# Two gated linear attentions in one decoder layer: how the scans' scores are placed and how the values are turned

## Chip, cores and metric

The kernel runs on one core of a Trainium2 chip. The metric is the device time of one execution in microseconds. Before the change the median of three runs is 2266.98 us (2266.93 to 2267.67). In what follows PE is TensorE, DVE is VectorE, ACT is ScalarE, POOL is GpSimd, and SP is the engine whose queue issues most loads.

## What is computed

One layer of a decoder for a prompt of 256 tokens and 8 samples of 4 new tokens (32 columns), 288 columns in all, at width 2048: a gated feed-forward part (FFN, inner width 5632), a mixer, and a second FFN, each between two norms. The mixer is a linear recurrence per head, four GLA heads (values 256 wide) and eight HGRN2 heads (values 128 wide):

```python
x = x + 0.5 * rmsnorm(swiglu(rmsnorm(x, g[0]), ffn1_w_in[l], ffn1_w_out[l]), g[1])
m, sg, sh = hybrid_mixer(rmsnorm(x, g[2]), ...)
x = x + rmsnorm(m, g[3])
x = x + 0.5 * rmsnorm(swiglu(rmsnorm(x, g[4]), ffn2_w_in[l], ffn2_w_out[l]), g[5])

# in the mixer, per head:
#   S_t = diag(exp(log_a_t)) S_{t-1} + k_t^T v_t ;  o_t = q_t S_t
```

The outputs are the layer's result for all tokens and the heads' new states.

## The kernel before

**Layout and matmuls.** Activations lie with features on the 128 partitions and the 288 tokens along the free axis: 16 tiles x (the residual), 16 tiles y (outputs of a part, later the heads' outputs), and xh and xl, the high and low halves of the normed input. Every large product is made of three matmuls of 288 columns (lines 548 to 550): high weights with both halves of the input, low weights with the high half. `block` does such a product for 512 output rows; a `tick` is called after each of its 16 steps over the inner dimension, that is after 12 matmuls. Weights come through SP in units of 128 x 1024; ACT copies the high half of a unit (wh, line 96) and DVE subtracts it from the raw one (wl, line 97).

**The mixer.** Its blocks in order are qk0, v0, qk1, v1 (GLA), hfq0, hi0, hfq1, hi1, hfq2, hfq3 (HGRN2), four gate blocks, and the output projection. A scan handles two heads; there are six scans (two GLA, four HGRN2). A scan is a Python generator; each tick of a later block runs one step of it (`step`), so its small operations stand between the block's matmuls in program order on each engine. A GLA scan skips the first four ticks of a block (SCAN_LAG). Each engine works through its own queue in that order.

**A scan.** The scores of a scan are built level by level (level lv pairs blocks of h = 2**lv tokens, masks and decay products F by `update`, lines 1022 to 1027). Step 0 makes own, the elementwise product of q and k at even tokens, in the tile rp, split in halves oh and ol. At step 2 `score01` sums own over the features by two 288-column matmuls with a matrix of ones (line 975, into sc_o) and makes levels 0 and 1 by `quarters` (line 959): blocks of 32 by 32 tokens on four column groups of PE. At step 3 `put01` moves them into Dg, the 2 x 2 tiles of 128 x 128 scores, by DVE's copy_predicated under the mask mk; `put_masked` (line 968) does one such copy for each of four partition blocks of 32, since each block's destination lies in other columns of Dg. At step 4 follow the sample scores into Ds (lines 1001, 1009) and `put23` (three times `put_masked`). Level 4 (h = 16) is copied by ACT (line 1080, four copies), levels 5 and 6 by ACT too (line 1086), level 7 into X. The steps with an extra yield are 3 to 6: scores are made at one tick and put at the next. After the levels come key_t, `out` (lines 1168 to 1178, the outputs from Vt, Dg, X, the states and Ds), the norm, the new states (line 1205) and their stores through POOL's queue (line 1207).

**The values.** A value block (v0, v1, hi0, hi1) leaves its product times rt in y tiles, and the 32 sample columns three times in v3 (lines 887, 888). Its four `turn`s wait in the list `turns`; one is taken at each tick of the next block from k = 1 on. A turn makes three PE transposes (`by_token`, lines 866 and 867) into tp_v; ACT copies the two prompt ones into Vt (line 895) and the sample one into V32 (line 896), and `stack` makes the high and low halves Vs (lines 871, 873).

**The other place that matters.** The last FFN turns its results already by `turn32` (line 660: DVE's block transposes of 32 x 32) and `move32` (lines 671, 675): 20 DMAs on POOL's queue put the blocks where a full transpose would have them.

Of the kernel before, what the change touches and what calls it, by code (L numbers as in the profile page):

```python
# [9 lines left out]
F32 = mybir.dt.float32  # L10
F32R = mybir.dt.float32r
# [5 lines left out]
P = 128  # L17
# [108 lines left out]
def trunk_kernel(ctx, tc, x_prompt, x_sample, state_gla, state_hgrn, norm_gains, f1_in, f1_out, f2_in, f2_out,  # L126
# [116 lines left out]
    y = [xpool.tile([P, T], F32, name=f"y{k}") for k in range(KT)]  # L243
# [532 lines left out]
    def mixer(pn, border):  # L776
        with ExitStack() as mx:
# [15 lines left out]
            mk = cst.tile([P, 576], U8, name="mk")  # L793
# [27 lines left out]
            def setup():  # L821
# [20 lines left out]
                G.tensor_copy(mk, mi32)  # L842
# [20 lines left out]
            def by_token(tp, src, src3):  # L863

                for t in range(2):
                    PE.transpose(tp[:, t * P:(t + 1) * P], src[:, t * P:(t + 1) * P], ident)
                PE.transpose(tp[0:96, TP:TP + P], src3, ident)
# [7 lines left out]
            def vtiles(nm):  # L875
                vs32.append(vs32.pop(0))
                return (gp.tile([P, 2, 512], F32, name=f"V{nm}", tag="V"), vs32[-1],
                        gp.tile([96, 512], F32R, name=f"Vs{nm}", tag="Vs"))
# [3 lines left out]
            def ev_v(Vt, V32, Vs, y0=8):  # L882
                def ev(f, ps):

                    vt = y[y0 + f]
                    v3 = tmp.tile([P, 3, TS], F32, name="v3", tag="v3", bufs=4)
                    V.tensor_tensor(vt[:, 0:TP], ps[:, 0:TP], rt[:, 0:TP], op=ALU.mult)
                    V.tensor_tensor(v3, ps[:, TP:T].unsqueeze(1).broadcast_to([P, 3, TS]),
                                    rt[:, TP:T].unsqueeze(1).broadcast_to([P, 3, TS]), op=ALU.mult)

                    def turn():
                        tp = auxtile("tp_v")
                        by_token(tp, vt, v3.rearrange("p n t -> p (n t)"))
                        c = slice(f * P, (f + 1) * P)
                        S.activation(Vt[:, 0:2, c], tp[:, 0:TP].rearrange("p (t c) -> p t c", c=P), AF.Copy)
                        S.activation(V32[0:TS, c], tp[0:TS, TP:TP + P], AF.Copy)
                        stack(Vs[:, c], tp, TS)

                    turns.append(turn)
                return ev  # L900
# [9 lines left out]
            def scan(d, Vt, V32, Vs, gla, ytile0, s0, sp_out, ss_out):  # L910
# [34 lines left out]
                oh = sp[0].tile([P, T], F32R, name="oh", tag="bd")  # L945
                ol = sp[0].tile([P, T], F32R, name="ol", tag="bd")
# [15 lines left out]
                def put_masked(src, h, m):  # L962

                    for b in range(4):
                        r = slice(b * TS, (b + 1) * TS)
                        dst = Dflat[r, :, r].rearrange("p j (n two k) -> p j n two k", two=2, k=h)[:, :, :, 1, :]
                        mv = mk[r, m * 64 + b * 16:m * 64 + (b + 1) * 16].rearrange("p (n k) -> p n k", k=h)
                        V.copy_predicated(dst, mv.unsqueeze(1).broadcast_to(dst.shape),
                                          src[r].rearrange("p j (n k) -> p j n k", k=h))

                def score01():

                    ps, po = auxtile("sc01"), auxtile("sc_o")
                    for i, part in enumerate((oh, ol)):
                        PE.matmul(po[:, 0:T], ones[128], part, start=i == 0, stop=i == 1, skip_group_check=True)
                    quarters(ps, lambda i, a, b: R[:, a, :, i * 64 + b * 16:i * 64 + (b + 1) * 16])
                    for a in range(2):
                        c = T + a * TS
                        PE.matmul(po[0:TS, c:c + TS], k[:, a, TP:T], R[:, a, :, P:P + TS // 2],
                                  start=False, stop=True, skip_group_check=True)  # L980
                    return ps, po

                def put01(ps, po):
                    def eye(n, m):
                        return mk[0:n, 448:448 + 2 * m].rearrange("p (n two) -> p n two", two=2)[:, :, 0]

                    def odd():
                        for lv in range(2):
                            put_masked(ps[:, 0:P].rearrange("p (j l c) -> p j l c", j=4, l=2)[:, :, lv], 1 << lv, lv)

                    def even():
                        v = Dflat.rearrange("p (i a) (n two) -> p i a n two", a=2, two=2)
                        ov = po[:, 0:T].rearrange("p (a c) -> p a c", a=2)
                        for i in range(2):
                            V.copy_predicated(v[:, i, :, :, 0], eye(P, 64).unsqueeze(1).broadcast_to([P, 2, 64]),
                                              ov[:, :, i * 64:(i + 1) * 64])

                    def sampled():
                        sv = Ds[0:TS].rearrange("p a (n two) -> p a n two", two=2)
                        ov = po[:, 0:T].rearrange("p (a c) -> p a c", a=2)  # L1000
                        V.copy_predicated(sv[:, :, :, 0], eye(TS, 16).unsqueeze(1).broadcast_to([TS, 2, 16]),
                                          ov[0:TS, :, P:])
                        for lv in range(2):
                            h = 1 << lv
                            m = mk[:, lv * 64:(lv + 1) * 64]
                            dst = Ds[0:TS].rearrange("p a (n two k) -> p a n two k", two=2, k=h)[:, :, :, 1, :]
                            for a in range(2):
                                c = T + a * TS + lv * 16
                                V.copy_predicated(dst[:, a], m[0:TS, 0:16].rearrange("p (n k) -> p n k", k=h),
                                                  po[0:TS, c:c + 16].rearrange("p (n k) -> p n k", k=h))  # L1010

                    return [odd, even, sampled]
# [60 lines left out]
                def put(lv, ps):  # L1073
# [17 lines left out]
                for step in range(LEVELS + 1):  # L1091
                    if step == 0:
                        V.scalar_tensor_tensor(own.unsqueeze(3), halves(q, 1, False), 128.0, halves(k, 1, False),
                                               op0=ALU.mult, op1=ALU.mult)
                        S.activation(oh, rp, AF.Copy)
                        V.tensor_tensor(Q, q, d["f"], op=ALU.mult)
                        V.tensor_tensor(ol, rp, oh.bitcast(F32), op=ALU.subtract)
# [425 lines left out]
```

## Time and profile before

| what | value |
|---|---|
| median of the runs shown | 2266.98 us |
| the profiled execution, its own time | 2267.07 us |
| its span, first to last instruction | 2265.0 us |
| mean granted TensorE clock | 0.998 |
| ACT busy, copies of wh (line 96) | 711.5 us |
| DVE busy, subtractions of wl (line 97) | 821.7 us |
| weights moved by SP's queue (q1) | 365.15 MB, 50.6% of 16 DMA engines |
| POOL's queue (q0) | 14.41 MB, 2.4% |

Busy times of different engines overlap. A row of a group gives line, engine, operation, out<-in, shapes and count; then busy time and the mean duration of one in ns; then the idle time of the engine just before such operations and what ended it. In a timeline a row is start, duration, engine, line, operation, and in brackets the wait ahead of it with its releaser. A PE row's duration is the latency of a matmul, not the step from one to the next, since matmuls are pipelined.

### The profile page before, as it was taken

The page shows a single profiled execution, that of the slowest core. Times are in us where ns is not written, and L with a number is a line of the kernel's source. Part 1 is how long each engine was busy: PE and PEld are TensorE (multiplying, and loading weights), DVE is VectorE, ACT ScalarE, POOL GpSimd, SP SyncE. Part 2 cuts the span into 40 slices and gives each one's busy share as a digit, 9 for nine tenths or more (in the row PEclk, how much of TensorE's full clock was granted, in tenths as well). Part 3 has the DMA queues.
Part 4 walks back from the last instruction along what each step waited for, and adds up shares of the span by engine and source line. Part 5 has one row for each costly group of instructions (what it writes and reads, how often), then busy time and mean ns, then how long its engine had stood idle before and what let it go on. Part 6 is the DMA issues. An engine that isn't in the chain of part 4 may idle for free. (4 is left out here: it accounts for less than half of the span.)

```text
span 2265.0 us, 43259 instructions
## 1 busy us (share of the span) xinstructions
PE 2244.5 (99%) x17760; PEld 2227.3 (98%) x17760; DVE 1409.0 (62%) x2359; ACT 1022.7 (45%) x1581; POOL 134.9 (6%) x241
## 2 busy tenths in 40 slices
PE   9999999999999999999999999999999999999998
PEld 9999999999999999999999999999999999999998
DVE  6545545554555468888889754954555455545546
ACT  6443333333334346555656654644333333333344
POOL 2000000000000001011000000440000000000005
PEclk9999999999999999999999999999999999999999
DMA  6555555555555554566555554565555555555545
GB/s 213 171 165 167 168 167 163 165 167 168 167 164 182 167 168 140 168 187 189 163 167 177 164 186 150 168 190 165 164 167 167 168 164 164 165 168 168 164 164 156
DMA packets 225605, 382.49 MB, mean 169 GB/s; under 512 B 20242, under 2 KB 60224, under 8 KB 225408
## 3 DMA queue, kind: packets, MB, share of 16 engines
q1 hardware_dynamic: 214736, 365.15, 50.6%
q0 software_dynamic: 8496, 14.41, 2.4%
q8 instruction: 139, 2.28, 0.4%
q10 hardware_dynamic: 2176, 0.18, 0.1%
q14 instruction: 58, 0.48, 0.1%
HBM read 363.75 MB, written 11.80 MB: 166 GB/s over the span
## 5 line engine op out<-in xcount | busy, mean ns | idle before, releaser
L97 DVE TENSOR_TENSOR wl<-raw,wh 128x1024 fp32r<-128x1024 f32 (+1 forms) x674 | 821.7, 1220 | 615.3 <-ACT wh L96 612.7
L96 ACT ACTIVATE wh<-raw 128x1024 fp32r<-128x1024 f32 (+1 forms) x674 | 711.5, 1057 | 1018.9 <-PE gate L549 313.7
L548 PE MATMUL gate<-xh,wh 128*128 128x288 f32 x1660 | 488.4, 296 | 0.6 <-ACT xh L254 0.6
L550 PE MATMUL gate<-xh,wl 128*128 128x288 f32 x1660 | 488.5, 295 | 0.4 <-DVE wl L97 0.4
L549 PE MATMUL gate<-xl,wh 128*128 128x288 f32 x1660 | 485.7, 295 | 0.6 <-DVE xl L255 0.6
L549 PE MATMUL out<-hl,wh 128*128 128x288 f32 x1408 | 415.7, 295 | 0.0
L550 PE MATMUL up<-xh,wl 128*128 128x288 f32 x1408 | 415.0, 295 | 0.0
L550 PE MATMUL out<-hh,wl 128*128 128x288 f32 x1408 | 415.0, 295 | 0.0
L548 PE MATMUL up<-xh,wh 128*128 128x288 f32 x1408 | 414.9, 295 | 0.0
L549 PE MATMUL up<-xl,wh 128*128 128x288 f32 x1408 | 414.6, 294 | 0.0
L548 PE MATMUL out<-hh,wh 128*128 128x288 f32 x1408 | 413.7, 294 | 0.0
L548 PEld LDWEIGHTS gate<-xh,wh 128*128 128x128 f32 x1660 | 310.9, 188 | 1.9 <-ACT xh L254 1.0
L550 PEld LDWEIGHTS gate<-xh,wl 128*128 128x128 f32 x1660 | 311.3, 188 | 1.1 <-DVE wl L97 0.8
L549 PEld LDWEIGHTS gate<-xl,wh 128*128 128x128 f32 x1660 | 310.4, 188 | 1.2 <-DVE xl L255 0.8
L550 PEld LDWEIGHTS out<-hh,wl 128*128 128x128 f32 x1408 | 264.7, 188 | 0.0
L548 PEld LDWEIGHTS out<-hh,wh 128*128 128x128 f32 x1408 | 264.6, 188 | 0.0
L549 PEld LDWEIGHTS out<-hl,wh 128*128 128x128 f32 x1408 | 264.4, 188 | 0.0
L548 PEld LDWEIGHTS up<-xh,wh 128*128 128x128 f32 x1408 | 264.1, 188 | 0.3
L549 PEld LDWEIGHTS up<-xl,wh 128*128 128x128 f32 x1408 | 264.2, 188 | 0.1
L550 PEld LDWEIGHTS up<-xh,wl 128*128 128x128 f32 x1408 | 264.2, 188 | 0.0
L706 DVE TENSOR_TENSOR y<-out,y 128x288 f32<-128x288 f32 x288 | 121.2, 452 | 101.3 <-PE out L550 98.3
L548 PE MATMUL hfq<-xh,wh 128*128 128x288 f32 x256 | 77.6, 304 | 0.0
(376 smaller groups left out, 2518.9 us busy)
## 6 DMA issues: line engine op xcount, KB each, us to landing
raw<-in_ffn_w_in_dram SPq DMA_DIRECT2D x351, 512.0 KB, 3.5
raw<-in_ffn_w_out_dram SPq DMA_DIRECT2D x176, 512.0 KB, 3.5
raw<-in_mix_w_in_dram SPq DMA_DIRECT2D x64, 512.0 KB, 3.8
raw<-in_mix_w_in_dram SPq DMA_DIRECT2D x96, 256.0 KB, 3.1
raw<-in_mix_w_out_dram SPq DMA_DIRECT2D x32, 512.0 KB, 3.6
out_dram<-s POOLq DMA_DIRECT2D x32, 256.0 KB, 2.8
s<-in_state_gla_dram SPq DMA_DIRECT2D x16, 256.0 KB, 4.2
s<-in_state_hgrn_dram SPq DMA_DIRECT2D x16, 256.0 KB, 4.2
```

The lines of the kernel that those rows point to most:

```text
L96: i1 = self.nc.scalar.activation(h[:, c], raw[:, c], AF.Copy).ins
L97: i2 = self.nc.vector.tensor_tensor(l[:, c], raw[:, c], h[:, c].bitcast(F32), op=ALU.subtract).ins
L548: yield lambda: PE.matmul(dst, w[0][:, c:c + P], parts[0], start=start, stop=False)
L549: yield lambda: PE.matmul(dst, w[0][:, c:c + P], parts[1], start=False, stop=False)
L550: yield lambda: PE.matmul(dst, w[1][:, c:c + P], parts[0], start=False, stop=stop)
L706: V.tensor_tensor(y[k], ps, y[k], op=ALU.add)
```

## The change

Three things move together.

- Masked copies: a new tile Db of 128 x 4 x 32 holds, for each partition block, only its own 32 columns. `put_masked` writes it for all 128 partitions in one copy, with masks rearranged so that each partition block finds its own 16 columns; the diagonal (even) scores and level 4 go the same way. At step 6, `place` copies Db into Dg by four ACT copies.
- score01: own is summed by matmuls with a 128 x 32 tile of ones, block by block, as the scores are; oh, ol and the tile sc_o go. All of it shares one PSUM tile.
- Values: for v0, v1 and hi0 the PE transposes are replaced by DVE block transposes into four y tiles that are free at that time (spare), and 20 DMAs on POOL's queue; then `parts` makes Vs from V32. hi1 has no spare tiles and keeps PE (`by_engine`). The 16 y tiles become four groups of four, Vt is laid out as [128, 4, 2, 128], and the entries of `turns` for a turned block are eight: two block transposes, four moves, an empty one, parts.

```diff
-    y = [xpool.tile([P, T], F32, name=f"y{k}") for k in range(KT)]
+    yg = [xpool.tile([P, 4, T], F32, name=f"y{k}") for k in range(4)]
+    y = [yg[k // 4][:, k % 4, :] for k in range(KT)]
...
-            mk = cst.tile([P, 576], U8, name="mk")
+            mk = cst.tile([P, 8, 16], U8, name="mk")
+            one32 = cst.tile([P, TS], F32, name="one32")
+            Db = cst.tile([P, 4, TS], F32, name="Db")
...
-                G.tensor_copy(mk, mi32)
+                G.memset(one32, 1.0)
+                G.memset(Db, 0.0)
+                for b in range(4):
+                    r = slice(b * TS, (b + 1) * TS)
+                    G.tensor_copy(mk[r, 0:7], mi32[r, 0:448].rearrange("p (l c) -> p l c", c=64)[:, :, b * 16:(b + 1) * 16])
+                    G.tensor_copy(mk[r, 7], mi32[r, 448 + b * TS:448 + (b + 1) * TS]
+                                  .rearrange("p (n two) -> p n two", two=2)[:, :, 0])
...
-            def ev_v(Vt, V32, Vs, y0=8):
+            def ev_v(Vt, V32, Vs, g, spare):
+                vg = yg[g]
+                if spare is not None:
+                    flat = yg[spare].rearrange("p f c -> p (f c)")
+                    b32 = flat[:, 0:4 * TP].rearrange("p (q n c) -> p q n c", q=4, c=TS)
+                    bs32 = flat[:, 4 * TP:].rearrange("p (f c) -> p f c", c=TS)
+                def by_engine(f):
+                    def run():
+                        tp = auxtile("tp_v")
+                        by_token(tp, vg[:, f, :])
+                        S.activation(Vt[:, f], tp[:, 0:TP].rearrange("p (t c) -> p t c", c=P), AF.Copy)
+                        S.activation(V32[0:TS, f * P:(f + 1) * P], tp[0:TS, TP:TP + P], AF.Copy)
+                    return run
+                def turn32(f):
+                    def run():
+                        for i in (f, f + 1):
+                            V.transpose(b32[:, :, 2 * i:2 * i + 2, :], vg[:, i, 0:TP].rearrange("p (t q c) -> p q t c", t=2, q=4))
+                        if f:
+                            V.transpose(bs32, vg[:, :, TP:T])
+                    return run
+                def move32(b, sample):
+                    rows = cols = slice(b * TS, (b + 1) * TS)
+                    def run():
+                        if sample:
+                            for n in range(4):
+                                r = slice(n * TS, (n + 1) * TS)
+                                G.dma_start(V32[0:TS].rearrange("p (f c) -> p f c", c=P)[:, :, r], bs32[r])
+                        for q in range(4):
+                            G.dma_start(Vt[q * TS:(q + 1) * TS, :, :, cols].rearrange("p f t c -> p (f t) c"), b32[rows, q])
+                    return run
+                def parts():
+                    v = V32[0:TS, :]
+                    S.activation(Vs[0:TS, :], v, AF.Copy)
+                    V.tensor_tensor(Vs[TS:2 * TS, :], v, Vs[0:TS, :].bitcast(F32), op=ALU.subtract)
+                    S.activation(Vs[2 * TS:96, :], v, AF.Copy)
                 def ev(f, ps):
...
+                    V.tensor_tensor(vg[:, f, :], ps, rt, op=ALU.mult)
+                    if spare is None:
+                        turns.append(by_engine(f))
+                    if f == 3:
+                        if spare is not None:
+                            turns.append(turn32(0))
+                            turns.append(turn32(2))
+                            turns.extend(move32(b, b == 0) for b in range(4))
+                            turns.append(lambda: None)
+                        turns.append(parts)
...
                 def put_masked(src, h, m):
-                    for b in range(4):
...
+                    dst = Db.rearrange("p j (n two k) -> p j n two k", two=2, k=h)[:, :, :, 1, :]
+                    mv = mk[:, m, :].rearrange("p (n k) -> p n k", k=h)
+                    V.copy_predicated(dst, mv.unsqueeze(1).broadcast_to(dst.shape),
+                                      src.rearrange("p j (n k) -> p j n k", k=h))
+                def place():
+                    for b in range(4):
+                        r = slice(b * TS, (b + 1) * TS)
+                        S.activation(Dflat[r, :, r], Db[r], AF.Copy)
                 def score01():
-                    ps, po = auxtile("sc01"), auxtile("sc_o")
-                    for i, part in enumerate((oh, ol)):
-                        PE.matmul(po[:, 0:T], ones[128], part, start=i == 0, stop=i == 1, skip_group_check=True)
+                    ps = auxtile("sc01")
                     quarters(ps, lambda i, a, b: R[:, a, :, i * 64 + b * 16:i * 64 + (b + 1) * 16])
+                    v = ps[:, P:P + 64].rearrange("p (i a c) -> p i a c", i=2, a=2)
                     for a in range(2):
+                        for b in range(4):
+                            PE.matmul(v[b * TS:(b + 1) * TS, :, a, :], one32,
+                                      own[:, a, 0:P].rearrange("p (i c) -> p i c", i=2)[:, :, b * 16:(b + 1) * 16],
+                                      start=False, stop=True, skip_group_check=True)
+                    for a in range(2):
+                        c = 192 + a * 16
+                        PE.matmul(ps[0:TS, c:c + 16], one32, own[:, a, P:P + 16],
+                                  start=False, stop=True, skip_group_check=True)
...
+                def put01(ps):
+                    for lv in range(2):
+                        put_masked(ps[:, 0:P].rearrange("p (j l c) -> p j l c", j=4, l=2)[:, :, lv], 1 << lv, lv)
+                    dst = Db.rearrange("p j (n two) -> p j n two", two=2)[:, :, :, 0]
+                    V.copy_predicated(dst, mk[:, 7, :].unsqueeze(1).broadcast_to(dst.shape),
+                                      ps[:, P:P + 64].rearrange("p (j c) -> p j c", j=4))
+                def put01_sample(ps):
+                    dst = Ds[0:TS].rearrange("p a (n two) -> p a n two", two=2)[:, :, :, 0]
...
+                    for lv in range(2):
...
+                        V.copy_predicated(dst, mv.unsqueeze(1).broadcast_to(dst.shape), src)
...
                     elif h == 16:
-                        for b in range(0, P, TS):
-                            S.activation(Dflat[b:b + h, :, b + h:b + TS],
-                                         ps[b:b + h, 0:64].rearrange("p (j c) -> p j c", j=4), AF.Copy)
+                        put_masked(ps[:, 0:64].rearrange("p (j c) -> p j c", j=4), h, lv)
...
                     if step == 0:
-                        V.scalar_tensor_tensor(own.unsqueeze(3), halves(q, 1, False), 128.0, halves(k, 1, False),
-                                               op0=ALU.mult, op1=ALU.mult)
-                        S.activation(oh, rp, AF.Copy)
+                        V.tensor_tensor(own.unsqueeze(3), halves(q, 1, False), halves(k, 1, False), op=ALU.mult)
                         V.tensor_tensor(Q, q, d["f"], op=ALU.mult)
-                        V.tensor_tensor(ol, rp, oh.bitcast(F32), op=ALU.subtract)
...
                         if step == 3:
-                            odd, even, sampled = put01(*pss.pop(1))
-                            odd()
-                            even()
+                            put01(pss[1])
                         elif step == 4:
-                            sampled()
+                            put01_sample(pss.pop(1))
                             put23(*pss.pop(3))
                         else:
                             put(step - 1, pss.pop(step - 1))
+                            if step == 6:
+                                place()
...
-                    block("v0", KT, xrhs, ev_v(*vt), 
+                    block("v0", KT, xrhs, ev_v(*vt, 2, 1), 
...
-                    block("v1", KT, xrhs, ev_v(*vt), tick=tick)
+                    block("v1", KT, xrhs, ev_v(*vt, 2, 1), tick=tick)
...
-                    block(f"hi{g}", KT, xrhs, ev_v(*vts[g], 8 + 4 * g), tick=tick)
+                    block(f"hi{g}", KT, xrhs, ev_v(*vts[g], 2 + g, None if g else 3), tick=tick)
```

More of the change, by code (lines that the diff above doesn't have):

```diff
@@ L861, in group_tiles, with by_token @@
                 return {n: gp.tile([P, 2, T], F32, name=f"{n}_{nm}", tag=n) for n in ("q", "k", "f")}
-            def by_token(tp, src, src3):
+            def by_token(tp, src, src3=None):
                 for t in range(2):
                     PE.transpose(tp[:, t * P:(t + 1) * P], src[:, t * P:(t + 1) * P], ident)
-                PE.transpose(tp[0:96, TP:TP + P], src3, ident)
+                n = TS if src3 is None else 3 * TS
+                PE.transpose(tp[0:n, TP:TP + P], src[:, TP:T] if src3 is None else src3, ident)
             def stack(dst, tp, low):
@@ L876, in vtiles @@
                 vs32.append(vs32.pop(0))
-                return (gp.tile([P, 2, 512], F32, name=f"V{nm}", tag="V"), vs32[-1],
+                return (gp.tile([P, 4, 2, P], F32, name=f"V{nm}", tag="V"), vs32[-1],
                         gp.tile([96, 512], F32R, name=f"Vs{nm}", tag="Vs"))
             turns = []
-            def ev_v(Vt, V32, Vs, y0=8):
-                def ev(f, ps):
[L885 to L899, printed above, removed]
```

54 lines of the change are left out of this document (14 added, 40 removed).

## The prediction

> **What bounds the kernel now.** I read the page's busy times first, then the windows over the mixer, then the PE and VectorE timelines around the places where PE stands.
>
> ```profile
> span 2265.0 us, 43259 instructions
> PE 2244.5 (99%) x17760; PEld 2227.3 (98%) x17760; DVE 1409.0 (62%) x2359; ACT 1022.7 (45%) x1581; POOL 134.9 (6%) x241
> ```
>
> PE works 99% of the span. So the time is the matmul stream plus its holes: an edit gains only if it takes instructions from PE or closes a hole, and anything on VectorE, ScalarE or GpSimd is free until PE waits for it. The holes of the mixer, where all of the change lies, show in windows laid over it (columns: microseconds, then busy time of PE, weight loads, DVE, ACT, POOL; five of fourteen windows and their sum):
>
> ```profile
> 1000.00:1030.00 30.00, 30.00 (x324) 28.50 (x324) 24.96 (x60) 19.37 (x44) 0.15 (x1) 1.00 0.64 194
> ...
> 1055.00:1085.00 30.00, 28.26 (x345) 26.89 (x343) 25.65 (x69) 15.16 (x39) 0.00 (x0) 1.00 0.61 175
> ...
> 1110.00:1130.00 20.00, 17.64 (x184) 16.44 (x184) 18.99 (x54) 9.23 (x27) 0.00 (x0) 1.00 0.45 137
> ...
> 1170.00:1215.00 45.00, 43.72 (x477) 41.97 (x476) 41.26 (x102) 28.50 (x69) 4.11 (x6) 1.00 0.57 171
> 1215.00:1260.00 45.00, 43.71 (x458) 42.19 (x457) 42.17 (x104) 28.67 (x68) 0.00 (x0) 1.00 0.54 161
> sum 435.00, PE 427.38 PEld 412.98 DVE 377.33 ACT 264.43 POOL 42.49; mean PE 30.53 PEld 29.50 DVE 26.95 ACT 18.89 POOL 3.03
> ```
>
> PE is short of full by 435.00 - 427.38 = 7.6 us, and nearly all of it (1.7, 2.4, 1.3, 1.3) lies in windows where DVE is busy 86 to 95%. Where DVE has air, as in 1000 to 1030, PE has no hole. What DVE does just ahead of two holes, and who waits, stands in the two timelines:
>
> ```profile
> 1114.45 3.04 DVE L968 COPY_PREDICATED Dg<-mk,sc 32x64 f32<-32x64 uint8 x12
> 1117.52 1.23 DVE L97 TENSOR_TENSOR wl<-raw,wh 128x1024 fp32r<-128x1024 f32 x1
> ...
> 1070.85 0.33 PE L1069 MATMUL sc<-Q,k_h 128*32 128x32 f32 x16 [1.30 <-DVE F L1027]
> ...
> 1118.80 0.40 PE L550 MATMUL hfq<-xh,wl 128*128 128x288 f32 x1 [0.34 <-DVE wl L97]
> ```
>
> Twelve masked copies in a row hold DVE for 3.04 us, the low half of a weight unit (wl) comes only behind them, and PE waits for it at 1118.8. At 1070.85 it waits 1.30 for a decay product that stands behind the same run of copies one scan earlier. The view of waits, PE's alone, adds them up (us in total, times, longest):
>
> ```profile
> PE sc L959 <- DVE k_h L1025: 2.6, 3, 1.2
> PE sc L1069 <- DVE F L1027: 1.6, 2, 1.3
> PE hfq L550 <- DVE wl L97: 1.2, 2, 0.8
> PE sc L959 <- DVE R L1038: 1.0, 2, 0.6
> ```
>
> These four are 6.4 us in nine waits, all of them on DVE. So two things can be had: PE's own small work, and these waits.
>
> **The change part by part. (a) Turns taken from PE.** Three of four value blocks (v0, v1, hi0) lose the PE transposes; hi1 keeps them. What a main matmul takes, and what one turn inserts, the PE timeline shows:
>
> ```profile
> 499.78 0.30 PE L549 MATMUL out<-hl,wh 128*128 128x288 f32 x1
> ...
> 503.88 0.30 PE L550 MATMUL out<-hh,wl 128*128 128x288 f32 x1
> ...
> 987.68 0.29 PE L550 MATMUL hfq<-xh,wl 128*128 128x288 f32 x1
> 987.82 0.38 PE L866 MATMUL tp_v<-ident,y 128*128 128x128 f32 x2
> 988.03 0.27 PE L867 MATMUL tp_v<-ident,v 128*96 128x128 f32 x1
> 988.06 0.38 PE L548 MATMUL hfq<-xh,wh 128*128 128x288 f32 x1
> 988.28 0.29 PE L549 MATMUL hfq<-xl,wh 128*128 128x288 f32 x1
> ```
>
> From 499.78 to 503.88 there are 31 steps: 4.10 / 31 = 0.132 us a matmul (the 0.29 is its latency). From 987.68 to 988.28 two matmuls should have taken 0.265 and took 0.60, so a turn costs PE 0.33 us. Four pieces in three blocks are twelve turns: 12 x 0.33 = **4.0 us less**. hi1's third transpose becomes narrower (32 for 96 columns of weights) but streams the same 128 columns: nothing.
>
> **(b) score01.** Out go two matmuls of 288 columns, in come 8 of 32 columns on four column groups and 2 of 16 columns; an f32 matmul leaves two records, so 16 + 4.
>
> ```profile
> 994.37 0.30 PE L550 MATMUL hfq<-xh,wl 128*128 128x288 f32 x1
> ...
> 994.63 0.29 PE L975 MATMUL sc_o<-ol,ones 128*128 128x288 f32 x1
> 994.86 0.46 PE L959 MATMUL sc<-R,k_g 128*32 128x32 f32 x32
> 995.13 0.29 PE L979 MATMUL sc_o<-R,k_g 128*32 128x32 f32 x4
> 995.35 0.40 PE L548 MATMUL hfq<-xh,wh 128*128 128x288 f32 x1
> ```
>
> The two wide ones cost 0.26. The 32 records of the same narrow form take 0.27 (994.86 to 995.13), so 16 more cost 0.14; four records on one column group take 0.22 at most (995.13 to 995.35), so the four half as long cost 0.1 to 0.2. That is -0.02 to +0.10 a scan; with the bounds set wider for an unseen mix, -0.6 to +1.5 for six scans. I take **0**, as the middle value is +0.2.
>
> **(c) The masked copies.** Each copy over four blocks of 32 partitions becomes one over 128. The forms in the mixer (last columns: busy, mean ns of one | idle before):
>
> ```profile
> L968 DVE COPY_PREDICATED Dg<-mk,sc 32x64 f32<-32x64 uint8 x120 | 30.4, 254 | 3.4
> L995 DVE COPY_PREDICATED Dg<-mk,sc_o 128x128 f32<-128x128 uint8 x12 | 4.4, 472 | 0.2
> L1009 DVE COPY_PREDICATED Ds<-mk,sc_o 32x16 f32<-32x16 uint8 x24 | 2.9, 180 | 0.0
> L873 DVE TENSOR_TENSOR Vsh<-tp_v,Vsh 32x128 fp32r<-32x128 f32 x8 | 2.3, 284 | 0.3
> L1027 DVE TENSOR_TENSOR F<-F 128x144 f32<-128x144 f32 x6 | 1.8, 305 | 0.0
> L1097 DVE TENSOR_TENSOR ol<-rp,oh 128x288 fp32r<-128x288 f32 x6 | 2.7, 450 | 0.0
> ```
>
> No masked copy of 128 x 64 is in the trace. Between the 32 x 64 (254 ns) and the 128 x 128 (busy 4.4 over 12, so 370 ns) it is bounded from both sides; since 32 x 128 and 128 x 144 tensor operations differ by 21 ns, partitions hardly count, and I take 254. Step 3 of a scan then goes from 8 x 254 + 2 x 370 = 2.8 us to 3 x 254 = 0.8. Step 4 goes from 12 x 254 + 4 x 120 + 0.2 = 3.7 (the four small ones are 2.9 / 24 each) to 3 x 254 + 0.2 + 2 x 0.2 = 1.4. The low half of the diagonal products (450 ns) goes; one copy (254) comes at step 5, for four on ACT. That is 2.0 + 2.3 + 0.45 - 0.25 = 4.5 us of DVE a scan, 27 us of the 377 in these windows, and it goes at the very points where the queue backs up. The runs of copies shrink by 2.0 and 2.3 us while the single waits behind them are 1.3 and less.
>
> What comes back: all of the 7.6 us, plus about 1.4 that the modelled matmul ends cover (0.29 - 0.13 = 0.16 in each of nine waits), is the upper bound, 9.0. The lower bound is 2, the case in which the update chain that stays on DVE, with wl among it, is late anyhow. I take **6.5**, the four rows of waits: the runs that went were longer than each of them. The rest is left where PE waits for ACT's copies of queries. ACT itself pays four diagonal copies (place) at step 6, four operations as it now does at h = 16, later and over 128 instead of 64 elements; PE reads them in out, at least four ticks on, and a tick is 12 x 0.132 = 1.6 us. Cover gone, it would be their length, under 1.2 us a scan.
>
> **(d) The new way of the values.** For a turned block ACT loses twelve operations and gets two, of 512 columns. DVE pays four block transposes of 411 ns, a shorter one and one subtraction of 512 columns where it had four operations of 284: at most 1.5 us more a block, spread over three ticks, against the 4.5 a scan that it is spared. GpSimd gets 20 DMAs a block. The final FFN already does exactly this:
>
> ```profile
> L660 DVE STREAM_TRANSPOSE b<-x 128x256 f32<-128x256 f32 x16 | 6.5, 411 | 0.0
> ...
> L671 POOL DMA_DIRECT2D xT<-b x64 | 37.2, 588 | 178.8 <-ACT sq L392 173.0 <-DVE bs L662 3.7 <-issue 0.8
> ...
> xT<-b POOLq DMA_DIRECT2D x64, 32.0 KB, 3.6
> xS<-bs POOLq DMA_DIRECT2D x16, 16.0 KB, 3.4
> ...
> 1450.00:1460.00 10.00, 10.00 (x76) 9.89 (x75) 7.38 (x12) 6.03 (x10) 9.54 (x18) 1.00 0.78 211
> ```
>
> Twenty issues of 0.59 are 11.7 us, and the last lands 3.6 later: 15.3 us after the first. The first reader on PE is out, the fifteenth step of the scan: with the moves from tick 3 on and a scan that starts at tick 0 at the earliest, 11 ticks or 17.5 us, plus what the steps themselves add. On ACT the first reader is the copy into Vs at tick 8: the four sample moves come first, 4 x 0.59 + 3.4 = 5.8 us, against 5 ticks, 8.0 us. From 1450 to 1460 GpSimd issued such moves without pause and PE was full: they cost PE **nothing** as long as both readers come later. What queues ahead of them on GpSimd are the state stores of the scan that ends; SP's weight loads are not passed. If the copy into Vs is late, the weight splits (wh) behind it on ACT are late with it.
>
> The Trainium skill ("DMA: Bandwidth & Descriptors", Rules for kernel authors) says to join many small transfers into a large one, as under 64 KB one pays mostly overhead. The trace agrees that 32 KB take 3.6 us to land, but the issues follow each other at 0.59, so the overheads overlap; what the rule would make of the sum if they did not is the last rival below.
>
> The extra set-up on GpSimd (masks cut in eight small copies, two fills) ends long before step 3 of the first scan and has only idle time around it.
>
> **Sum.** The profiled execution took 2267.07 us with a span of 2265.0; the median shown is 2266.98, so 0.1 less. 2267.0 - 4.0 + 0 - 6.5 = **2256.5 us**.
>
> **The rivals.** First, **the holes stay**: what PE waits for is the update chain, not the copies, and with 1.2 us wl operations between them DVE stays late. For it: at 1118.8 the wait is on wl itself. Against it: DVE is 4.5 us a scan lighter just there. Then only (a) and the lower bound of 2 (or nothing) count: 2261 to 2263.
>
> Second, **everything closes**: 2267.0 - 4.0 - 9.0 = 2254.
>
> Third, on the other side, **the values come late**. Place: the copy into Vs on ACT at tick 8, which waits for DMAs that wait for the block transposes on a crowded DVE. The slack is 8.0 - 5.8 = 2.2 us. If DVE is late by two runs like that from 1114.45 (3.04 + 1.23 = 4.3, twice 8.6), ACT stands 6.4 us in each of three blocks, weight splits and the scan's own copies with it; were PE to stand as long, 3 x 6.4 = 19 us come on top: 2276. It is slower than before from 3.5 us of standing a block on. Against it: the copies that make DVE late are what shrinks.
>
> Fourth, **the moves don't overlap**: each of 20 waits for the one before to land, 20 x 3.6 = 72 us; out would wait 72 - 17.5 = 54 us in three blocks, 2256.5 + 160 = about 2420. The 0.59 us between issues speaks against it. (This is where the rule on small transfers, taken as a serial cost, would lead.)
>
> **How the numbers follow.** The forecast (6.5 of the holes, within 2.5) has 0.58, everything closes 0.13, the holes stay 0.20, the values late 0.08, no overlap 0.01. The range runs from the everything-closes case with the lower bound of (b), 2253, to the holes-stay case with a little of (b)'s upper one, 2263.5. A measurement of this kernel tells about 0.2%, 4.5 us, from no change. Forecast, all-closed and most of the holes-stay case are faster than that: 0.86. Within 0.2% fall the case with no hole closed at all and a mild lateness: 0.08. Slower 0.06.
>
> **What would show it.** In the profile after: the tp_v groups with a third of their instructions (8 and 4, besides hi1's narrower form); masked copies of 128 x 64 at about 254 ns, some 42 in place of 120; DVE down by about 27 us over the mixer; PE busy within 2 us of full in the windows above; the moves of the values on GpSimd at 0.59 us, with no wait of ACT's Vs copies or of PE's out for a DMA. I am wrong if the 128-partition copies take 400 ns or more, if holes remain behind the update chain, or if ACT's row for Vs waits for a DMA by more than 2 us.

## The result and the profile after

| | us |
|---|---|
| before, median of 4 runs | 2267.32 (2266.93 to 2268.95) |
| after, median of 4 runs | 2257.18 (2256.98 to 2259.15) |
| ratio, with its 95% interval | 0.9957 (0.9942 to 0.9972) |
| profiled execution after, its own time | 2256.99 |

The change made the kernel 10.1 us faster in these runs; 10.5 were forecast. Measured once more in the second set of experiments (further down), it was 6.9 us faster, so the last few microseconds of the agreement are luck. The page of the kernel after begins:

```profile
span 2255.2 us, 43315 instructions
PE 2240.6 (99%) x17832; PEld 2224.7 (99%) x17832; DVE 1378.3 (61%) x2238; ACT 1018.9 (45%) x1543; POOL 170.1 (8%) x310
```

The span is 9.8 us shorter and DVE is 31 us less busy; POOL is 35 us busier, which is the 60 moves. The windows over the mixer, laid as before (same columns, then granted clock, DMA share, GB/s):

```profile
1000.00:1030.00 30.00, 30.00 (x267) 28.62 (x266) 22.68 (x45) 20.90 (x52) 1.65 (x3) 1.00 0.63 194
...
1055.00:1085.00 30.00, 27.57 (x297) 26.34 (x296) 20.19 (x52) 17.88 (x44) 5.98 (x10) 0.94 0.54 150
...
1110.00:1130.00 20.00, 20.00 (x199) 19.29 (x199) 12.68 (x21) 12.12 (x29) 0.00 (x0) 1.00 0.55 165
...
1170.00:1215.00 45.00, 45.00 (x451) 43.64 (x451) 37.05 (x80) 32.05 (x78) 4.10 (x6) 1.00 0.56 165
1215.00:1260.00 45.00, 45.00 (x458) 43.47 (x457) 36.04 (x84) 28.31 (x65) 2.81 (x4) 1.00 0.62 180
sum 435.00, PE 432.04 PEld 418.62 DVE 352.06 ACT 266.18 POOL 78.09; mean PE 30.86 PEld 29.90 DVE 25.15 ACT 19.01 POOL 5.58
```

Three of the four windows in which PE had holes are full now. The fourth, 1055 to 1085, got worse (28.26 before, 27.57 now), though DVE in it is down from 25.65 to 20.19, and its clock is 0.94. It holds 2.4 of the 3.0 us that PE still misses. The view of PE's waits names what it is (us in total, times, longest):

```profile
PE sc L1005 <- ACT R L1080: 2.4, 1, 2.4
...
PE sc L1005 <- ACT R L996: 0.3, 1, 0.3
```

All waits of the scans on DVE are gone, and one on ACT is new. ACT's timeline around it:

```profile
1053.58 0.27 ACT L1158 ACTIVATE acc<-k_h 128x96 f32<-128x96 f32 x1
1056.24 0.63 ACT L933 ACTIVATE Vsh<-vs 32x512 fp32r<-32x512 f32 x1 [2.39 <-DMA vs<-y]
1056.88 0.63 ACT L935 ACTIVATE Vsh<-vs 32x512 fp32r<-32x512 f32 x1
1057.53 0.41 ACT L1080 ACTIVATE R<-Q 128x256 f32<-128x256 f32 x1
```

ACT stands 2.39 us at the copy into Vs, until the sample moves of hi0's values have landed, and the copy of queries (R) comes behind both copies into Vs. R's own input was there long before, as DVE's timeline shows:

```profile
1054.13 0.42 DVE L1065 TENSOR_TENSOR Q<-Q,F 128x256 f32<-128x256 f32 x1
```

So R could have run at 1054.55 and ran at 1057.53. What PE makes of it, with the first matmul of the mixer's first unit (qk) and of the one behind its last scan (mo), in PE's timeline after:

```profile
852.64 0.38 PE L549 MATMUL qk<-fill2xh,wh 128*128 128x288 f32 x1
...
1058.00 0.29 PE L1005 MATMUL sc<-R,k_h 128*32 128x48 f32 x8 [2.43 <-ACT R L1080]
...
1059.12 0.44 PE L551 MATMUL hfq<-xh,wl 128*128 128x288 f32 x1
1059.36 0.44 PE L549 MATMUL hfq<-xh,wh 128*128 128x288 f32 x1
...
1295.34 0.29 PE L549 MATMUL mo<-xh,wh 128*128 128x288 f32 x1
```

Behind the wait a main matmul takes 0.24 us a step (1059.12 to 1059.36) in place of 0.13. The windows laid over it say why:

```profile
1055.00:1058.00 3.00, 0.57 (x6) 0.34 (x4) 0.26 (x3) 1.73 (x4) 2.04 (x4) 1.00 1.12 282
...
1059.00:1060.00 1.00, 1.00 (x6) 1.00 (x5) 0.97 (x4) 0.00 (x0) 1.00 (x3) 0.50 0.92 213
1060.00:1061.00 1.00, 1.00 (x6) 1.00 (x5) 1.00 (x2) 0.00 (x0) 0.73 (x2) 0.50 0.52 94
```

PE is busy 0.57 of 3 us, and then its granted clock is 0.50: PE counts as fully busy there and does half the work. Such a stretch costs time that the view of waits doesn't show.

**The measure used from here on** is the length of the mixer on PE, from the first matmul of qk to the first of mo. The same two rows of the kernel before:

```profile
854.15 0.38 PE L548 MATMUL qk<-fill2xh,wh 128*128 128x288 f32 x1
...
1305.55 0.29 PE L548 MATMUL mo<-xh,wh 128*128 128x288 f32 x1
```

Before it is 1305.55 - 854.15 = 451.4 us, after 1295.34 - 852.64 = 442.7: 8.7 us less. Another 1.5 us of the difference between the two profiles lie ahead of qk (854.15 against 852.64), where only set-up on GpSimd was changed; in ten profiles of this study qk begins between 852.6 and 857.2, also at different times for the same kernel. The length leaves that out. It comes from one profile of each kernel, and of the changed kernel there are two, 442.7 and 441.4; so a difference of a few tenths is not more than a hint, above all between kernels with a stretch at half clock.

The rows of the operations that the prediction priced: groups of DVE over the mixer, then one of ACT,

```profile
L1012 DVE COPY_PREDICATED Db<-mk,sc 128x64 f32<-128x64 uint8 x36 | 8.8, 245 | 0.1
L914 DVE STREAM_TRANSPOSE y<-y 128x256 f32<-128x256 f32 x12 | 4.7, 420 | 0.0
...
L1043 DVE COPY_PREDICATED Db<-mk,sc 128x64 f32<-128x64 uint8 x6 | 1.8, 296 | 0.0
```

```profile
L1018 ACT ACTIVATE Dg<-Db 32x128 f32<-32x128 f32 x24 | 7.4, 307 | 7.1 <-DVE Db L1012 6.9
```

and of the tile of turns on PE (count, then least, median and most ns):

```profile
L877 PE MATMUL tp_v<-ident,y x8: 270/272/329, 1111.8 to 1118.1; 128*128 128x128 f32 x8
...
L879 PE MATMUL tp_v<-ident,y x4: 272/272/273, 1112.0 to 1118.2; 128*32 128x128 f32 x4
```

### The profile page after: what moved, and what is told of

Read it like the earlier page. It is cut to its first block, busy times and chain, and to the rows that moved or that the text cites. A ratio compares the mean times of both kernels' runs of the same rounds, so it can differ in the third digit from the quotient of the medians.

```text
span 2255.2 us, 43315 instructions
## 1 busy us (share of the span) xinstructions
PE 2240.6 (99%) x17832; PEld 2224.7 (99%) x17832; DVE 1378.3 (61%) x2238; ACT 1018.9 (45%) x1543; POOL 170.1 (8%) x310
## 4 chain that ended last, share of the span: by engine, by line
PE 97%; DVE 1%; ACT 1%; issue 0%; DMA 0%; POOL 0%; DVEq 0%; ACTq 0%; POOLq 0%
PE gate L549 10%; PE gate L551 10%; PE gate L550 10%; PE up L551 8%; PE up L549 8%; PE up L550 8%; PE out L550 8%; PE out L551 8%; PE out L549 8%; PE mo L551 2%; PE mo L549 2%; PE mo L550 2%; PE hfq L549 1%; PE hfq L551 1%; PE hfq L550 1%; PE qk L549 1%
```

## The experiments

Two sets, each on one chip beside the kernel before: the four rows under "after" are the first set, the last four the second. All times are medians with lowest and highest; the ratio is to the kernel before of the same set (2267.62 and 2267.46 us). The row "after" repeats the result above, with its own measurement of the kernel before (2267.32). The length is that of the mixer, from one profile.

| kernel | time, us | ratio (95%) | qk to mo, us |
|---|---|---|---|
| before | 2267.62; 2267.46 | 1 | 451.4 |
| after | 2257.18 | 0.9957 (0.9942 to 0.9972) | 442.7 |
| moves, Vs copy later by ticks | 2258.53 (2256.65 to 2261.24) | 0.9963 (0.9950 to 0.9975) | 442.6 |
| moves, Vs copy earlier | 2259.42 (2256.95 to 2262.35) | 0.9966 (0.9954 to 0.9978) | 442.8 |
| PE turns, wide copies | 2260.21 (2258.77 to 2261.29) | 0.9968 (0.9956 to 0.9981) | 442.6 |
| moves, split copies | 2271.42 (2267.98 to 2273.42) | 1.0016 (1.0007 to 1.0024) | 455.0 |
| moves, Vs copy behind R | 2255.10 (2254.74 to 2257.77) | 0.9947 (0.9935 to 0.9960) | 438.8 |
| the changed kernel again | 2260.59 (2257.20 to 2261.93) | 0.9966 (0.9954 to 0.9979) | 441.4 |
| moves, Vs copy behind R, hi1 by moves too | 2253.51 (2252.89 to 2256.37) | 0.9943 (0.9930 to 0.9955) | 437.6 |
| PE turns, split copies | 2269.69 (2266.89 to 2270.78) | 1.0008 (0.9999 to 1.0017) | 451.2 |

### The copy into Vs, later and earlier by ticks

My theory was that the new hole comes from where the copy into Vs stands; the rival, that DVE or the moves themselves are what is late. Later by three empty entries of `turns`:

```diff
-                            turns.append(lambda: None)
+                            turns.extend([lambda: None] * 4)
```

> The changed kernel with three more empty entries ahead of parts, so that ACT copies V32 into Vs at tick 11 and not at tick 8. Theory (values late): in the changed kernel ACT stood 2.4 us for the sample moves in the block after hi0, PE stood 2.4 us for ACT's copy R behind it, and ran at half clock for some 3.3 us after that, about 4.2 us in all. With three ticks (4.8 us) more the wait is gone: 2257.2 - 4.2 = 2253.0, no PE wait on R over 0.5 us, clock 1.00 there. Rival (the hole is the scan's own chain on DVE and ACT): 2257.2, the hole stays.

Earlier, behind the third move:

```diff
-                            turns.extend(move32(b, b == 0) for b in range(4))
-                            turns.append(lambda: None)
+                            turns.extend(move32(b, b == 0) for b in range(3))
                         turns.append(parts)
+                        if spare is not None:
+                            turns.append(move32(3, False))
```

> The changed kernel with parts at tick 6, two ticks (3.2 us) earlier, the last four moves after it. Theory (values late): ACT's wait grows by up to 3.2 us in each turned block; in the block after hi0 PE's hole grows from 2.4 to between 4 and 5.6 us, the blocks after v0 and v1 may show one too: 2259 to 2264. Rival (the scan's own chain): no change, 2257.2.

PE's waits with the later copy, then with the earlier one:

```profile
PE sc L1005 <- ACT R L1080: 2.5, 1, 2.5
```

```profile
PE sc L1006 <- ACT R L1081: 2.5, 1, 2.5
```

Neither moved anything: the same wait, the same length within 0.1 us, so what I called the theory was missed both times. On ACT the copy into Vs stands just ahead of the same R in both. So the place in the list of entries didn't decide the order on ACT, although the text on the kernel before says that each engine works in program order. What does decide it (perhaps the order in which the compiler reckons instructions ready) no run shows. The experiments said nothing yet on what the hole costs, and my argument by ticks had lost its ground.

### The turns back on PE, the wide copies kept

```diff
-ev_v(*vt, 2, 1)
+ev_v(*vt, 2, None)
...
-ev_v(*vts[g], 2 + g, None if g else 3)
+ev_v(*vts[g], 2 + g, None)
```

> The changed kernel with all four value blocks turned by PE as hi1 is; masked copies and score01 as changed. Theory: against the kernel of e1 twelve turns of 0.33 us come back, 4.0 us, and the holes on DVE stay closed: 2253.0 + 4.0 = 2257.0, no more PE waits on DVE over 0.5 us than the changed kernel has. Rival (the holes closed because turns left ACT, DVE and PSUM, not because of the copies): holes of 3 us and more return, 2260 to 2265.

Its PE timeline, and its group of wide copies on DVE:

```profile
855.60 0.38 PE L549 MATMUL qk<-fill2xh,wh 128*128 128x288 f32 x1
...
1298.23 0.29 PE L549 MATMUL mo<-xh,wh 128*128 128x288 f32 x1
```

```profile
L1012 DVE COPY_PREDICATED Db<-mk,sc 128x64 f32<-128x64 uint8 x36 | 8.8, 244 | 0.2
```

442.6 us, as long as the changed kernel in its first profile (its second, below, is 1.2 us shorter). The time expected, 2257.0, was missed (2260.21), since it rested on the 2253.0 of the later copy; no wait of the scans on DVE is back, so the theory on the holes held. All of the change without the moves brings 451.4 - 442.6 = 8.8 us, and moving twelve turns away from PE, as the change does it, next to nothing.

### The small copies back, with the moves and with the turns on PE

With the later copy into Vs and with the turns on PE, levels 0 to 3 are again copied in blocks of 32 partitions; the diagonal, level 4 and score01 stay as changed:

```diff
-                    dst = Db.rearrange("p j (n two k) -> p j n two k", two=2, k=h)[:, :, :, 1, :]
+                    for b in range(0, P, TS if h < 16 else P):
+                        r = slice(b, b + (TS if h < 16 else P))
+                        dst = Db[r].rearrange("p j (n two k) -> p j n two k", two=2, k=h)[:, :, :, 1, :]
...
```

> The kernel of e1, but put_masked writes levels 0 to 3 into Db in four copies of 32 partitions each, so the 120 small copies are back on DVE (20 a scan for 5, about 3.8 us a scan more); all else as in e1. Theory (copies make the holes): 5 to 9 us of holes return, 2258 to 2262, with PE waits on DVE in the scans of HGRN2. Rival (something else closed them): under 2 us more than e1, 2253 to 2255.

> The kernel of e3 (all turns by PE) with the copies of levels 0 to 3 in four of 32 partitions each, so that of the change only score01 and the copies of the diagonal and of level 4 are left. Theory (copies make the holes): 7 to 9 us over e3's 553.4 from qk to mo, 560 to 562, near the kernel before. Rival (the 12 us of e4 came from the block transposes and Vs on DVE, not from the copies): under 4 us over e3.

In the second of these expectations and in the three that follow, the lengths near 553 us (and 549, 548 and 560) rest on a wrong subtraction of mine; the changed kernel's length is 442.7. What can be compared are the differences in them. Waits, PE's timeline and the copies of the kernel with turns on PE and split copies:

```profile
PE sc L1005 <- DVE k_h L1070: 2.4, 4, 0.9
...
PE hi L549 <- DVE z L1400: 1.4, 1, 1.4
...
PE hfq L551 <- DVE wl L97: 0.8, 1, 0.8
PE sc L1114 <- DVE F L1072: 0.8, 1, 0.8
```

```profile
856.94 0.38 PE L549 MATMUL qk<-fill2xh,wh 128*128 128x288 f32 x1
...
1308.13 0.29 PE L549 MATMUL mo<-xh,wh 128*128 128x288 f32 x1
```

```profile
L1014 DVE COPY_PREDICATED Db<-mk,sc 32x64 f32<-32x64 uint8 x120 | 30.4, 253 | 3.2
```

Its length is 451.2, that of the kernel before within 0.2 us, and the waits on k_h, wl and F are back, with one on z that the kernel before doesn't have. So everything else that this kernel keeps of the change (score01, the diagonal, level 4, `place`, the copies into Vs) is worth 0.2 us on balance, and the split of the copies alone 451.2 - 442.6 = 8.6 us: 120 small copies of 253 ns against 30 of 244. That is the clean reading, one edit between two kernels, though on two chips; the ratios to the kernel before on each (1.0008 and 0.9968) differ by as much, 0.4%. Of the 8.6 us, 6.8 are idle time of PE between qk and mo (7.2 against 0.4) and 1.8 are time in which the profile counts PE as busy (444.0 against 442.3).

With the moves the same edit costs 455.0 - 442.6 = 12.4 us, more than the 5 to 9 expected. The hole at R grew there to 3.1 us, PE waits 1.5 us more on k_g, which the kernel with PE turns doesn't, and the half-clock stretch behind R shows in the windows:

```profile
1066.00:1070.00 4.00, 4.00 (x39) 3.88 (x32) 3.39 (x12) 0.49 (x1) 2.48 (x6) 0.50 0.46 96
```

Four microseconds at a clock of 0.50 are 2 us lost, and the stretch is longer than this window. This kernel, moves with the old copies, is slightly slower than before (1.0016, 1.0007 to 1.0024): without the wide copies the moves, as the change does them, would have been a loss.

### The copy into Vs ordered behind R

`tc.issue_after` fixes the order of issue on an engine and adds no wait:

```diff
-                    S.activation(Vs[0:TS, :], v, AF.Copy)
-                    V.tensor_tensor(Vs[TS:2 * TS, :], v, Vs[0:TS, :].bitcast(F32), op=ALU.subtract)
-                    S.activation(Vs[2 * TS:96, :], v, AF.Copy)
+                    with tc.issue_after(near_copy[0]) if near_copy[0] else ExitStack():
+                        S.activation(Vs[0:TS, :], v, AF.Copy)
+                        V.tensor_tensor(Vs[TS:2 * TS, :], v, Vs[0:TS, :].bitcast(F32), op=ALU.subtract)
+                        S.activation(Vs[2 * TS:96, :], v, AF.Copy)
...
-                    S.activation(near, src, AF.Copy)
+                    near_copy[0] = S.activation(near, src, AF.Copy).ins
```

> The changed kernel with one more rule of order on ACT: the two copies into Vs are issued behind the copy R of the scan's third step (L1080 of the changed kernel), where e1 and e2 showed that moving them in the program left their place on ACT as it was. Theory (values late): ACT copies R without waiting for the sample moves, so PE's hole of 2.4 us and the half-clock stretch after it go: from the first qk matmul to the first mo matmul 553.4 - 4.0 = 549.4 us, the time 4 us under the changed kernel on the same chip. Rival (the hole is the scan's own chain, R late by itself): the hole stays in place, 553 us. Second rival (the wait moves to the weight splits behind Vs): part of the 4 us comes back as PE waits on wl.

The changed kernel was run beside it again, unchanged:

> The changed kernel once more, as the measure for e5 and e7 on the same chip: 553.4 us from the first qk to the first mo matmul, with the hole at R; the time 2257 to 2259.

ACT's timeline with the order fixed, then PE's:

```profile
1059.17 0.42 ACT L1081 ACTIVATE R<-Q 128x256 f32<-128x256 f32 x1 [0.74 <-DVE Q L1066]
...
1061.03 0.63 ACT L934 ACTIVATE Vsh<-vs 32x512 fp32r<-32x512 f32 x1 [0.30 <-DMA vs<-y]
```

```profile
857.21 0.38 PE L549 MATMUL qk<-fill2xh,wh 128*128 128x288 f32 x1
...
1295.96 0.29 PE L549 MATMUL mo<-xh,wh 128*128 128x288 f32 x1
```

R goes as soon as its input is there, ACT's stand shrinks from 2.39 to 0.30 us, and PE waits for nothing at this place. The length is 438.8: 4.0 less than the changed kernel in its first profile, and 3.9 less than the kernel with its turns on PE. So the twelve turns are worth what a turn was priced at, once the copy into Vs is out of R's way. Neither rival came true. The times of the set agree: 2255.10 against 2260.59 (2257 to 2259 had been expected of the second), and without the slowest run of the first the two ranges lie apart.

The changed kernel's second profile has the hole and not the half clock:

```profile
PE sc L1005 <- ACT R L1080: 2.6, 1, 2.6
```

```profile
1060.00:1061.50 1.50, 1.50 (x25) 1.44 (x12) 1.44 (x6) 0.49 (x1) 1.50 (x3) 1.00 0.99 246
```

The clock is 1.00 right behind the hole, and the length 441.4, 1.3 us shorter than in its first profile. That splits the 4.0 us: about 2.7 for the hole itself (441.4 - 438.8), about 1.3 for the slow stretch, which comes in some executions. PE's times agree: from qk to mo it is idle for 3.0 and 3.1 us in the two profiles, and busy for 439.7 and 438.3. The execution profiled is the shortest of its five, 2257.20; what made the others up to 4.7 us longer, this stretch or the part ahead of the mixer, no profile shows.

### hi1 by moves too

With four more tiles (`xtra`) to turn into, the last block can go the same way, on top of the order behind R:

```diff
+            xtra = cst.tile([P, 4, T], F32, name="xtra")
...
-                    flat = yg[spare].rearrange("p f c -> p (f c)")
+                    flat = (xtra if spare == 4 else yg[spare]).rearrange("p f c -> p (f c)")
...
-                    block(f"hi{g}", KT, xrhs, ev_v(*vts[g], 2 + g, None if g else 3), tick=tick)
+                    block(f"hi{g}", KT, xrhs, ev_v(*vts[g], 2 + g, 4 if g else 3), tick=tick)
```

> The kernel of e5 with hi1 turned by blocks and moves too, into a tile of its own of 128 x 4 x 288. Four PE turns go, 1.3 us. In the block after hi1 its scan reaches out about 16 us after the first turn, and 20 moves with their landing take 15.3 us from the third tick on. Theory (the moves are free only while their readers come later): out waits for the moves, 1 to 5 us, so the gain is lost or worse, 549 to 553 us from qk to mo. Rival (they fit): 548.1 us.

```profile
856.81 0.38 PE L549 MATMUL qk<-fill2xh,wh 128*128 128x288 f32 x1
...
1294.36 0.29 PE L549 MATMUL mo<-xh,wh 128*128 128x288 f32 x1
```

437.6 (the rows are PE's timeline): 1.2 less than the kernel it was built on, and no wait of PE's for a move. Four turns at 0.33 are 1.3. So the theory was missed and the rival came true. At 2253.51 us (ratio 0.9943, 0.9930 to 0.9955) it has the lowest median of the study, 14 us below before in its set; its range overlaps that of the kernel it was built on.

## Why the prediction was right, and by what

The time was right (2256.5 forecast, 2257.18 measured), and that it came so close is luck: of the sum behind it one term was too small, another was put at nothing and was not, the two errors pull opposite ways, and variation ahead of the mixer made up most of the rest. In the second set the same kernel came out 6.9 us under before (2260.59 against 2267.46). Term by term, on the length of the mixer:

| term | forecast | measured | from |
|---|---|---|---|
| (a) twelve turns | -4.0 | -3.9 | turns on PE, 442.6, to Vs behind R, 438.8 |
| (b) score01, with all else but copies and moves | 0 | -0.2 | before, 451.4, to PE turns with split copies, 451.2 |
| (c) wide copies, the holes | -6.5 | -8.6 | split to wide, turns on PE |
| (d) the moves | 0 | +4.0 | Vs behind R, 438.8, to the changed kernel, 442.7 (second profile: 441.4, +2.7) |
| sum | -10.5 | -8.7 | 451.4 to 442.7 |
| ahead of the mixer | 0 | -1.5 | 854.15 to 852.64 |
| from mo to the end | 0 | +0.4 | 959.45 to 959.86 (span less the start of mo) |

The last three lines add up to the difference of the spans, 2265.0 - 2255.2 = 9.8; the two executions' own times differ by 0.3 more, 2267.07 - 2256.99 = 10.1, outside the span. The part from mo to the end is 0.4 to 0.8 us longer than before in all nine profiles of changed kernels; why, no run shows.

**(a) held.** The price of a turn out of one gap in the timeline, 0.33 us, is confirmed twice, with twelve (3.9 us) and with four of them (1.2 us). The twelve show as PE's busy time between qk and mo: 442.3 with the turns on PE, 438.2 without.

**(b) held**, within its bounds of -0.6 to +1.5, as far as the runs show: no run changes score01 alone, and the -0.2 is a balance of all that the kernel with split copies keeps.

**(c) was right in mechanism and too small.** The copy over 128 partitions takes 245 ns (254 taken, 400 would have refuted it): over partitions it is free. The diagonal copy, of the same shape, takes 296. DVE is down by 377.33 - 352.06 = 25.3 us in the windows (27 forecast). The mis-sized step is the choice of 6.5 between 2 and 9: I took the four rows of waits that I showed and let the part that the modelled matmul ends cover stay. The view has three more rows of the scans on DVE, 1.1 us together:

```profile
PE sc L959 <- DVE Dg L968: 0.6, 1, 0.6
...
PE sc L1069 <- DVE k_h L1025: 0.3, 1, 0.3
...
PE sc L959 <- DVE r L1248: 0.2, 1, 0.2
```

Measured, 8.6, all but 0.4 of the upper bound of 9.0 went. The covered part was real time too: 1.8 us of the 8.6 were counted as busy PE. The rival "the holes stay" fell: not one wait of the scans on DVE is left. `place`, priced at nothing on ACT, has 307 ns a copy, and no wait of PE's leads to it.

**(d) failed at a step, and the third rival came true in one block of three.** The prediction gave the sample moves 5.8 us to land against 8.0 us until ACT comes to the copy, a slack of 2.2. POOL's timeline and the DMA issues in the window 1046 to 1064 (KB each, median us from issue to landing) show both figures:

```profile
1048.68 2.19 POOL L926 DMA_DIRECT2D vs<-y  x4
```

```profile
Vh<-y POOLq DMA_DIRECT2D x16, 32.0 KB, 5.3
...
vs<-y POOLq DMA_DIRECT2D x4, 16.0 KB, 5.1
```

ACT reached the copy at 1053.85 (1056.24 less its wait of 2.39), 5.2 us after the first issue and not 8.0, and the moves had landed 7.6 after it and not 5.8: the slack was -2.4. The first miss is the premise that the order on ACT follows the ticks, which the two experiments with the entries refuted. It decided the matter: had ACT come to the copy 8.0 us after the first issue, the moves landed after 7.6 would have been in time. The second is the landing time, read from the final FFN (3.4 us), where DMA share was 0.78; at this place it is over 1 (1.12 in the window 1055 to 1058), and landing takes 5.1. The price that the rival was given, 19 us, supposed a DVE late by 8.6 us; DVE was not late, and only the queueing on ACT was. In the blocks after v0 and v1 together ACT waits 3.3 us for the moves and PE does not notice. That "PE full beside such moves" was read off the final FFN was right as far as it went: PE lost nothing to the moves, but to what was queued behind one of their readers. By the prediction's own test (ACT's row for Vs waiting over 2 us) this step was wrong.

The 1.5 us ahead of the mixer come and go with the execution. They lie in the first 40 us, where PE is busy for 37.3 us before and for 38.8 after, but for 37.5 in the changed kernel's second profile. At 20 us DVE waits there for a block of the input (xb) to land: 1.90 us before, 0.51 after, 1.31 in the second profile. The same kernel's qk began at 852.64 and 854.08. What stays open is what sets the order of instructions on ACT.

## What to carry to other kernels

Where an engine backs up behind runs of small operations, count its instructions and not their elements: here 120 copies of 32 partitions took four times as long as 30 copies of 128. The stall behind them was worth more than the rows of the view of waits add up to, since part of it was counted as busy PE. When work moves from an engine to DMAs, look at the first instruction that reads the DMA's result: here everything queued behind it on its engine waited too (R for 3 us). It belongs behind whatever the bottleneck needs next, and here only an order rule put it there, not its place in the program. Price a transfer by rows from a stretch that is as full of transfers as the place it goes to.

## What the runs showed of the hardware

A hole of some 2.4 us on PE was enough for a stretch at half clock: after holes of 2.4, 2.5, 2.5 and 3.1 us (the changed kernel, the two with the Vs copy moved by ticks, the split copies) the granted clock fell to 0.50, in the changed kernel for about 3.2 us (1058.5 to 1061.7); after the 2.6 us hole of the changed kernel's second profile it stayed at 1.00. Before, where no wait in the scans was longer than 1.3 us, it was 1.00 in all the windows shown. Two shorter holes close together did it too: in the first FFN, between 22 and 26 us, the kernels with the Vs copy behind R, with hi1 by moves and with PE turns and split copies have waits of 1.4 to 1.9 us and of 0.6 with a matmul or two between, and a mean clock of 0.91 from 20 to 40 us; the kernels with PE turns and with moves and split copies have 1.5 and 0.6 there and stay at 1.00. The Trainium skill ("TensorE: Matmul & The Clock Gate", What's actually happening) has the clock halved after an idle window of about 3.4 us that runs free of the kernel. The half rate and the dependence on the execution agree with the trace; the length doesn't quite, as a hole of 2.4 us, with six matmul records in the 3 us around it, sufficed here.

A second one: where POOL issued moves of 16 to 32 KB back to back, they followed each other every 0.55 to 0.61 us, but their landing went from 3.4 us in the final FFN to 5.1 and 5.3 where the DMA engines were full. There POOL also stood between moves, 1.44 us ahead of 1055.96 until one had landed, so that the block's 20 issues took 14.2 us (1048.07 to 1062.25) and not the 11.7 of the forecast.
